# Six row buffers for the f32 expert blocks of a decoder layer, a norm diagonal on GpSimd, and key halves placed behind the norm

## The chip, the cores and the metric

The kernel runs on one core of a Trainium2 chip. What counts is device time in microseconds from start to end of one execution. The kernel before takes 1702.3 us (median of three runs, 1701.36 to 1702.61). All rows of a trace come from one other execution, run under the profiler, that took 1700.27 us; times in rows count from its first instruction.

## The reference

One decoder layer: 512 tokens, width 1024, float32, one batch. The layer mixes tokens (a gated recurrence beside a sparse attention), adds the result to the residual stream, sends the normed stream through an expert mixer with 16384 experts, of which each token uses 16 for each of 8 heads, and adds a gated embedding. Cut to what matters here:

```python
def rmsnorm(x, g):
    y = x32 * lax.rsqrt(jnp.mean(x32 * x32, axis=-1, keepdims=True) + EPS)
    return (y * g.astype(jnp.float32)).astype(x.dtype)

def peer_ffn(h, wq, sub_keys, u, v):
    def token_block(xt):                                  # 128 tokens
        q = (xt @ wq).reshape(PEER_TOKEN_BLOCK, PEER_HEADS, 2, PEER_DKEY // 2)
        s = jnp.einsum('thcd,hckd->thck', q, sub_keys)
        top_s, top_i = lax.top_k(s, PEER_TOPK)
        cand = top_s[:, :, 0, :, None] + top_s[:, :, 1, None, :]
        best_s, best_c = lax.top_k(cand.reshape(...), PEER_TOPK)
        ...                                               # expert = i1 * 128 + i2
        w = jax.nn.softmax(best_s, axis=-1)
        act = jax.nn.gelu(jnp.einsum('thkd,td->thk', u[expert], xt))
        return jnp.einsum('thk,thkd->td', w * act, v[expert])

        mixed = jnp.concatenate([o_hg, o_nsa], axis=-1)
        h = h + mixed @ w_out[i]
        h = h + peer_ffn(rmsnorm(h, ffn_norm[i]), peer_wq[i], peer_keys[i], peer_u[i], peer_v[i])
        gate = jax.nn.sigmoid(rmsnorm(h, ple_gate_norm[i]) @ ple_gate_w[i])
        h = h + (p[i] @ ple_proj[i]) * gate
```

## The kernel before, in words

The 512 tokens are four tiles of 128 (`tt` 0 to 3). A float32 product that must be exact is split: ScalarE writes a rounded high half of an operand, VectorE subtracts it from the operand to get the low half (`split`, L190), and TensorE adds up three matmuls of halves (`mm3`, L185). In the names `aTh` and `aTl` (`xTh` and `xTl` in the code) are the halves of the normed stream, `wh` and `wl` those of a chunk of the query weights, `kyh` and `kyl` those of the sub keys, `uh` and `ul` those of 128 rows of the expert table `u`, and `moh` and `mol` those of one tile of the attention output, transposed.

The work comes in stages. Up to about 347 us run the input projection, the recurrence, and the attention with most of its output projection. What the list `POST` (L73) then orders is the junction that the change edits. The letter "o" (`out_tile`, L518) transposes tile 0 of the attention output (L522), splits it, multiplies it with the output weights in two column halves of 12 matmuls, adds each half to the residual `h1` (L540) and sums its squares on ScalarE. The letter "n" (`ffn_norm`, L545) norms one tile: GpSimd computes the factor `rx` (three small instructions, L547, L180, L181), VectorE makes a 128x128 diagonal `dg` of it (L550, one buffer), TensorE multiplies the tile with it, which scales and transposes at once (L555), and ScalarE and VectorE write the halves `aTh` (L560) and `aTl` (L561).

Next, 16 steps (`hc`) multiply the normed stream with a chunk of the query weights each; at steps 0, 4, 8 and 12 a quarter of the sub keys is loaded into `kr_` and split (L940 to L943), and VectorE takes the 16 best scores of each key half. Tile 0 takes its experts one by one later; tiles 1 to 3 take all 16384 experts densely, in 128 blocks of 128 rows of `u`. Blocks 0 to 29 are worked on early. Six run after the last score; the others are spread between the one-hot matmuls (`wm`, L1036 and L1037) of three dense tiles, which turn the routing into a dense weight table (`wd`). Blocks 0 to 19 are "full": TensorE multiplies the float32 rows `ur` with the float32 stream `xf` (L834). Blocks 20 to 29 take the split rows `uh`, `ul` in three matmuls. The pool `dense` (L795) has two buffers of each name, 512 KB each, so two of `ur`, two of `uh` and two of `ul`; full blocks leave the last four empty. Loads of `ur` stand in SyncE's queue, apart from the last three of the 30, which GpSimd issues. Then the main loop runs over the 128 blocks (split rows of `u` and `v`, and for tile 0 gathered rows), and the gate ends the kernel.

Each engine works through its own instructions in order. Within a stage a scheduler lays the order by priorities; `tc.issue_after` puts instructions behind a given one.

Of the kernel before, what the change touches and what calls it, by code (L numbers as in the profile page):

```python
# [10 lines left out]
F32 = mybir.dt.float32  # L11
# [58 lines left out]
HPLAN = [("h", 0), ("h", 1), ("kv", 0), ("h", 2), ("h", 3)]  # L70
KPLAN = [("q", 0), ("k", 0), ("k", 1), ("s", 0), ("s", 1), ("s", 2), ("s", 3), ("c", 0)]
PLAN = [("b",0),("b",1),("c",),("a",3,(1,2,0),4),("p",),("a",3,(1,2,0),8),("a",3,(1,2,0),ALL),("l",0),("o",0,2),("o",0,0),("o",0,1),("a",2,(1,2,0),5),("a",2,(1,2,0),ALL),("o",0,3),("l",1),("a",1,(1,0,2),ALL),("o",1,3),("o",1,2),("a",0,(1,0,2),3),("a",0,(1,0,2),ALL),("o",1,1)]
POST = [("n",3),("o",0),("n",2),("n",1),("n",0)]  # L73
APRI = 150
XB = 6
NP = 3
# [83 lines left out]
def _body(ctx, tc, a, out, dbg=None):  # L160
# [354 lines left out]
            w.append((wh, wl))  # L515
        return w

    def out_tile(pool, pp, tag, bufs, w, hf, tt):  # L518
        src = (hv, nq)[hf]
        o = pp.tile([128, 512], F32, name=tag, bufs=bufs)  # L520
        for k in range(4):
            PE.transpose(o[:, k * 128:(k + 1) * 128], src[:, tt, k * 128:(k + 1) * 128], ident)  # L522
        mh = pool.tile([128, 4, 128], F32R, name="moh", bufs=MB)
        ml = pool.tile([128, 4, 128], F32R, name="mol", bufs=MB)
        split(flat(mh), flat(ml), o)
        outer = not hf and tt == LAST0
        os_ = [pp.tile([128, 512], F32, name=tag, bufs=bufs) for _ in range(2)] if outer else []
        for k in range(4 if outer else 0):
            for n in range(2):
                ns = slice(n * 512, (n + 1) * 512)  # L530
                mm3(os_[n], mh[:, k], ml[:, k], w[k][0][:, ns], w[k][1][:, ns], k == 0, k == 3)
        for n in range(2):
            ns = slice(n * 512, (n + 1) * 512)
            if outer:
                o = os_[n]
            else:
                o = pp.tile([128, 512], F32, name=tag, bufs=bufs)
                for k in range(4):
                    mm3(o, mh[:, k], ml[:, k], w[k][0][:, ns], w[k][1][:, ns], k == 0, k == 3)
            V.tensor_tensor(h1[:, tt, ns], h1[:, tt, ns], o, op=ALU.add)  # L540
            if hf:
                junk = pool.tile([128, 512], F32, name="junk")
                act(junk, h1[:, tt, ns], AF.Square, accum_out=ss[:, tt, n:n + 1])

    def ffn_norm(pool, pp, tag, bufs, tt):  # L545
        ts = slice(tt * 128, (tt + 1) * 128)
        G.tensor_tensor(rx[:, tt:tt + 1], ss[:, tt, 0:1], ss[:, tt, 1:2], op=ALU.add)  # L547
        rstd(rx[:, tt:tt + 1], rx[:, tt:tt + 1], 1, 1.0 / D)
        dg = pool.tile([128, 128], F32, name="dg", bufs=DGB)
        V.tensor_scalar(dg, ident, rx[:, tt:tt + 1], None, op0=ALU.mult)  # L550
        for q in range(2):
            o = pp.tile([128, 512], F32, name=tag, bufs=bufs)
            for k in range(4):
                c = 4 * q + k
                PE.matmul(o[:, k * 128:(k + 1) * 128], lhsT=h1[:, tt, c * 128:(c + 1) * 128], rhs=dg, start=True, stop=True)  # L555
            for k in range(4):
                c = 4 * q + k
                gc = gn[:, G_FFN + c:G_FFN + c + 1]
                ok = o[:, k * 128:(k + 1) * 128]
                act(xTh[:, c, ts], ok, AF.Copy, scale=gc)  # L560
                V.scalar_tensor_tensor(xTl[:, c, ts], ok, gc, xTh[:, c, ts].bitcast(F32), op0=ALU.mult, op1=ALU.subtract)  # L561

    dram = ctx.enter_context(tc.tile_pool(name="dram", bufs=1, space=DRAM))
    ppd = dram.tile([T, D], F32, name="ppd")
# [226 lines left out]
    wp = wpx.enter_context(tc.tile_pool(name="wp", bufs=2, reuse_waits="tile"))  # L791
    with ExitStack() as e2:
        ps = e2.enter_context(tc.tile_pool(name="ps2", bufs=6, space=PSUM, reuse_waits="tile"))
        for name, tt in POST:
            if name == "n":  # L795
                ffn_norm(wop, ps, "mm", 6, tt)
            else:
                out_tile(wop, ps, "mm", 6, wo_, 1, tt)
        put("h1", h1)
        wox.close()  # L800
        den = ExitStack()
        dense = den.enter_context(tc.tile_pool(name="dense", bufs=2, side="right", reuse_waits="tile"))
        pre = ExitStack()
        prep = pre.enter_context(tc.tile_pool(name="prep", bufs=AHEAD, side="right", reuse_waits="tile"))
# [14 lines left out]
    def a_steps(full):  # L819
        b = nextb[0]  # L820
        nextb[0] += 1
        dq = nc.gpsimd if NPRE - HOLD <= b < NPRE else nc.sync
        ur = dense.tile([128, NC, 128], F32, name="ur")
        dq.dma_start(out=ur, in_=a["uT"][b])
        g_ = prep.tile([128, TD], F32, name="gp") if b < AHEAD else dense.tile([128, TD], F32, name="ga", bufs=3)
        ahead.append(g_ if b < AHEAD or b >= NPRE else None)
        if not full:
            uh = dense.tile([128, NC, 128], F32R, name="uh")
            ul = dense.tile([128, NC, 128], F32R, name="ul")
            split(flat(uh), flat(ul), flat(ur))  # L830
        o = aps.tile([128, 512], F32, name="apsum")
        for c in range(NC):
            if full:
                PE.matmul(o[:, :TD], lhsT=ur[:, c], rhs=xf[:, c], start=c == 0, stop=c == NC - 1)  # L834
            else:
                mm3(o[:, :TD], uh[:, c], ul[:, c], xTh[:, c, T - TD:], xTl[:, c, T - TD:], c == 0, c == NC - 1)
            if c < NC - 1:
                yield
        act(g_, o[:, :TD], AF.Gelu_apprx_tanh)
        if AHEAD <= b < NPRE:  # L840
            dq.dma_start(out=gd[b - AHEAD], in_=g_)
# [76 lines left out]
    with ExitStack() as e2:  # L918
# [4 lines left out]
        with ExitStack() as e3:  # L923
            ps = e3.enter_context(tc.tile_pool(name="ps3", bufs=6, space=PSUM, reuse_waits="tile"))
            e3.enter_context(wpx)
            qs = []
            for hc in range(17):
                if hc == 4:
                    for c in range(NC):
                        G.tensor_tensor(xf[:, c], xTh[:, c, T - TD:].bitcast(F32), xTl[:, c, T - TD:].bitcast(F32), op=ALU.add)  # L930
                if hc < 16:
                    raw = wp.tile([128, NC, 128], F32, name="wr")
                    nc.sync.dma_start(out=raw, in_=a["wq"][:, hc])
                    wh = wp.tile([128, NC, 128], F32R, name="wh")
                    if hc == 0:
                        kyh = wp.tile([128, 16, 128], F32R, name="kyh", bufs=1)
                        kyl = wp.tile([128, 16, 128], F32R, name="kyl", bufs=1)
                    wl = wp.tile([128, NC, 128], F32R, name="wl")
                    split(flat(wh), flat(wl), flat(raw))
                    if hc % 4 == 0:  # L940
                        kr_ = wp.tile([128, 4, 128], F32, name="kr_")
                        nc.sync.dma_start(out=kr_, in_=a["keys"][:, hc:hc + 4])
                        split(kyh[:, hc:hc + 4], kyl[:, hc:hc + 4], kr_)  # L943
                    o = ps.tile([128, 512], F32, name="mm")
                    for c in range(NC):
                        mm3(o, wh[:, c], wl[:, c], xTh[:, c], xTl[:, c], c == 0, c == NC - 1)
                    qh = wp.tile([128, T], F32R, name="qh")
                    ql = wp.tile([128, T], F32R, name="ql")
                    split(qh, ql, o)
                    qs.append((qh, ql))  # L950
                if hc:
                    h = hc - 1
                    qh, ql = qs[h]
                    o = ps.tile([128, NT, 128], F32, name="mm")
                    for tt in range(NT):
                        ts = slice(tt * 128, (tt + 1) * 128)
                        last = mm3(o[:, tt], qh[:, ts], ql[:, ts], kyh[:, h], kyl[:, h], True, True)
                    for tt in range(NT):
                        V.max(tv[tt][:, h, 0:8], o[:, tt])
                        V.max_index(ti[tt][:, h, 0:8], tv[tt][:, h, 0:8], o[:, tt])  # L960
                        rep = wp.tile([128, 128], F32, name="rep")
                        V.match_replace(out=rep, in_to_replace=tv[tt][:, h, 0:8], in_values=o[:, tt], imm_value=-3e38)
                        V.max(tv[tt][:, h, 8:16], rep)
                        V.max_index(ti[tt][:, h, 8:16], tv[tt][:, h, 8:16], rep)
            with tc.issue_after(last.ins):
                for _ in range(XB):
                    a_block(True)
# [321 lines left out]
```

## Time and profile before

| What | us |
|---|---|
| median of three runs | 1702.3 |
| the profiled execution | 1700.27 |
| its span, first to last instruction | 1698.5 |
| TensorE busy / VectorE busy | 1650.0 / 1260.3 |
| ScalarE busy / GpSimd busy | 745.3 / 486.1 |

The profiled execution lies 2.0 us below the median, and 1.8 us of it are outside the span. PE is TensorE's matmuls, PEld its weight loads, DVE is VectorE, ACT is ScalarE, POOL is GpSimd and SP is SyncE. Busy shares are means over stages with different limits, so a change in one stage is read from that stage. A float32 matmul shows as more than one record in the trace: the eight of one tile's norm are the "x16" of L555.

### The profile page before, as it was taken

How to read it: one execution, taken by the hardware profiler on the slowest of the kernel's cores; microseconds unless marked ns; L12 is line 12 of the kernel's file. 1: busy time of each engine (PE TensorE's matmuls, PEld its weight loads, DVE VectorE, ACT ScalarE, POOL GpSimd, SP SyncE). 2: the span in 40 equal slices, each digit the busy share in tenths (PEclk: the TensorE clock that was granted, in tenths of full speed). 3: DMA queues.
4: the chain of work that ended last, by engine and by line, in shares of the span. 5: the costliest groups of instructions: out<-in, count | busy, mean ns of one | idle time of the engine just before them, and what ended most of it. 6: DMA issues, size and time to landing. Idle time of an engine off the chain costs nothing.

```text
span 1698.5 us, 24123 instructions
## 1 busy us (share of the span) xinstructions
PE 1650.0 (97%) x8864; PEld 1416.2 (83%) x8864; DVE 1260.3 (74%) x2485; ACT 745.3 (44%) x1291; POOL 486.1 (29%) x356
## 2 busy tenths in 40 slices
PE   9999999979999999999999999999999999999998
PEld 7887888768866668878899999999999999888987
DVE  6565745659999987865487877777878877787864
ACT  7443664652237875533333333333333333433342
POOL 0013000020000000000055655655545544455610
PEclk9999999989999999999999999999999999999999
DMA  7311130032214689967589898898898988899941
GB/s 256 112 50 49 45 100 25 26 101 86 63 50 146 203 259 287 309 222 239 171 302 327 309 337 313 323 331 325 318 324 323 322 318 322 319 329 333 328 140 50
DMA packets 148647, 373.38 MB, mean 220 GB/s; under 512 B 11990, under 2 KB 59734, under 8 KB 148526
## 3 DMA queue, kind: packets, MB, share of 16 engines
q1 hardware_dynamic: 109808, 231.46, 40.4%
q0 software_dynamic: 38720, 140.38, 23.3%
q8 instruction: 69, 1.13, 0.3%
q14 instruction: 50, 0.41, 0.1%
HBM read 339.02 MB, written 32.77 MB: 219 GB/s over the span
## 4 chain that ended last, share of the span: by engine, by line
PE 50%; issue 17%; DMA 15%; POOL 9%; DVE 5%; ACT 3%; SPq 0%; POOLq 0%; DVEq 0%; ACTq 0%
POOL row L1093 8%; DMA row<-v,eid 7%; PE ac L188 5%; PE ac L186 5%; PE ac L187 5%; PE mm L186 4%; PE mm L187 4%; PE mm L188 4%; PE apsum L834 3%; DMA ur<-uT 3%; DMA row<-u,eid 3%; PE apsum L188 3%; PE apsum L186 3%; PE apsum L187 3%; PE ob L708 2%
## 5 line engine op out<-in xcount | busy, mean ns | idle before, releaser
L188 PE MATMUL ac<-vh,pl 128*128 128x512 f32 x768 | 301.9, 394 | 1.9 <-DVE pl L192 1.7
L1093 POOL DMA_INDIRECT row<-u,eid x128 | 216.2, 1689 | 304.3 <-DVE hn L1097 246.3
L187 PE MATMUL ac<-vl,ph 128*128 128x512 f32 x768 | 301.1, 392 | 0.5 <-DVE vl L192 0.5
L186 PE MATMUL ac<-vh,ph 128*128 128x512 f32 x768 | 299.4, 391 | 1.9 <-ACT vh L191 1.0
L188 PE MATMUL apsum<-aTh,ul 128*128 128x384 f32 x864 | 290.4, 336 | 3.9 <-DVE ul L192 3.9
L186 PE MATMUL apsum<-aTh,uh 128*128 128x384 f32 x864 | 291.5, 337 | 0.5 <-ACT uh L191 0.5
L187 PE MATMUL apsum<-aTl,uh 128*128 128x384 f32 x864 | 289.6, 335 | 0.0
L1093 POOL DMA_INDIRECT row<-v,eid x128 | 208.8, 1631 | 184.0 <-DVE hn L1105 160.4
L191 ACT ACTIVATE uh<-ur 128x1024 fp32r<-128x1024 f32 x108 | 114.5, 1060 | 248.5 <-PE apsum L187 230.1
L192 DVE TENSOR_TENSOR ul<-ur,uh 128x1024 fp32r<-128x1024 f32 x108 | 132.1, 1223 | 78.5 <-ACT uh L191 78.3
L1105 DVE SCALAR_TENSOR_TENSOR hn<-row,cw__7013,hn 128x1024 f32<-128x1024 f32 x128 | 158.6, 1281 | 21.9 <-DMA row<-v,eid 21.7
L188 PEld LDWEIGHTS ac<-vh,pl 128*128 128x128 f32 x768 | 144.1, 188 | 34.8 <-DVE pl L192 4.8
L191 ACT ACTIVATE ph<-ga 128x384 fp32r<-128x384 f32 x118 | 62.0, 525 | 249.3 <-DVE ga L1154 194.6
L186 PEld LDWEIGHTS ac<-vh,ph 128*128 128x128 f32 x768 | 144.4, 188 | 30.7 <-ACT ph L191 2.2
L187 PEld LDWEIGHTS ac<-vl,ph 128*128 128x128 f32 x768 | 144.3, 188 | 29.2 <-DVE vl L192 1.2
L192 DVE TENSOR_TENSOR vl<-vr,vh 128x1024 fp32r<-128x1024 f32 x128 | 156.0, 1219 | 16.0 <-ACT vh L191 16.0
L188 PEld LDWEIGHTS apsum<-aTh,ul 128*128 128x128 f32 x864 | 162.8, 188 | 5.2 <-DVE ul L192 5.2
L191 ACT ACTIVATE vh<-vr 128x1024 fp32r<-128x1024 f32 x128 | 135.2, 1056 | 71.3 <-PE ac L188 70.4
L186 PEld LDWEIGHTS apsum<-aTh,uh 128*128 128x128 f32 x864 | 162.8, 188 | 4.5 <-ACT uh L191 0.6
L187 PEld LDWEIGHTS apsum<-aTl,uh 128*128 128x128 f32 x864 | 162.8, 188 | 3.9
L1097 DVE SCALAR_TENSOR_TENSOR hn<-row,hn 128x1024 f32<-128x1024 f32 x128 | 156.2, 1221 | 3.3 <-DMA row<-u,eid 1.8
L834 PE MATMUL apsum<-xf,ur 128*128 128x384 f32 x320 | 114.7, 503 | 9.5 <-DMA ur<-uT 9.5
(403 smaller groups left out, 2902.7 us busy)
## 6 DMA issues: line engine op xcount, KB each, us to landing
vr<-v SPq DMA_DIRECT2D x128, 512.0 KB, 5.4
ur<-uT SPq DMA_DIRECT2D x125, 512.0 KB, 6.4
xf<-wd SPq DMA_DIRECT2D x30, 768.0 KB, 8.3
wraw<-wi SPq DMA_DIRECT2D x20, 512.0 KB, 4.8
wd<-hn SPq DMA_DIRECT2D x5, 1664.0 KB, 8.7
wd<-stage SPq DMA_DIRECT2D x5, 1664.0 KB, 9.3
wr<-wq SPq DMA_DIRECT2D x16, 512.0 KB, 3.6
wor<-wo SPq DMA_DIRECT2D x16, 256.0 KB, 2.7
```

The lines of the kernel that those rows point to most:

```text
L186: PE.matmul(o, lhsT=lh, rhs=rh, start=first, stop=False)
L187: PE.matmul(o, lhsT=lh, rhs=rl, start=False, stop=False)
L188: return PE.matmul(o, lhsT=ll, rhs=rh, start=False, stop=last)
L191: act(hi, src, AF.Copy)
L192: return V.tensor_tensor(lo, src, hi.bitcast(F32), op=ALU.subtract)
L708: PE.matmul(o_ps[:, h], lhsT=pt[:, k * 128:(k + 1) * 128], rhs=kv[:, k, 256 + i * 64:256 + (i + 1) * 64], start=(k == 0), stop=(k == tt))
L834: PE.matmul(o[:, :TD], lhsT=ur[:, c], rhs=xf[:, c], start=c == 0, stop=c == NC - 1)
L1093: G.indirect_dma_start(out=gt, out_offset=None, in_=table, in_offset=bass.IndirectOffsetOnAxis(ap=eid[:, slot:slot + 1], axis=0))
L1097: V.scalar_tensor_tensor(junk, gt, 1.0, xn0, op0=ALU.mult, op1=ALU.mult, accum_out=dots[:, s_:s_ + 1])
L1105: V.scalar_tensor_tensor(ak, gt, cw_[:, s_:s_ + 1], ak, op0=ALU.mult, op1=ALU.add)
```

## The change

Four edits. The diagonal is made on GpSimd in place of VectorE. `POST` starts with a new letter "t": the transposes of tile 0 and their split (`out_turn`) come ahead of the norm of tile 3, and `out_tile` later uses their result. All four key splits are issued behind the last `aTl` of the norm. The row buffer of a full block takes the names `ur`, `uh`, `ul` in turn. (`WLP` is 99, a step that doesn't exist, so its branch is never taken.)

```diff
-POST = [("n",3),("o",0),("n",2),("n",1),("n",0)]
+DGG = 1
+KYP = 16
+WLP = 99
+POST = [("t",0),("n",3),("o",0),("n",2),("n",1),("n",0)]
...
-    def out_tile(pool, pp, tag, bufs, w, hf, tt):
+    def out_turn(pool, pp, tag, bufs, hf, tt):
         src = (hv, nq)[hf]
...
         split(flat(mh), flat(ml), o)
+        return mh, ml
+
+    def out_tile(pool, pp, tag, bufs, w, hf, tt, turned=None):
+        mh, ml = turned or out_turn(pool, pp, tag, bufs, hf, tt)
...
-        V.tensor_scalar(dg, ident, rx[:, tt:tt + 1], None, op0=ALU.mult)
+        (G if DGG else V).tensor_scalar(dg, ident, rx[:, tt:tt + 1], None, op0=ALU.mult)
...
-                V.scalar_tensor_tensor(xTl[:, c, ts], ok, gc, xTh[:, c, ts].bitcast(F32), op0=ALU.mult, op1=ALU.subtract)
+                normed[0] = V.scalar_tensor_tensor(xTl[:, c, ts], ok, gc, xTh[:, c, ts].bitcast(F32), op0=ALU.mult, op1=ALU.subtract)
...
+            elif name == "t":
+                turned = out_turn(wop, ps, "mm", 6, 1, tt)
             else:
-                out_tile(wop, ps, "mm", 6, wo_, 1, tt)
+                out_tile(wop, ps, "mm", 6, wo_, 1, tt, turned)
...
-        ur = dense.tile([128, NC, 128], F32, name="ur")
+        ur = dense.tile([128, NC, 128], F32, name=("ur", "uh", "ul")[b % 3] if full else "ur")
...
-                        split(kyh[:, hc:hc + 4], kyl[:, hc:hc + 4], kr_)
+                        if hc < KYP:
+                            with tc.issue_after(normed[0].ins):
+                                split(kyh[:, hc:hc + 4], kyl[:, hc:hc + 4], kr_)
...
```

How it moves instructions shows at three places. On TensorE, where the junction begins, the order before has the norm of tile 3 (mm_3390, mm_3403), then the transposes (mm_3416), and the two halves of the output projection (mm_3425, mm_3441) start mixed, with the norm of tile 2 (mm_3462) between them:

```order
L555 MATMUL mm_3390<-dg_3388,h1_63 128x128 x4
L555 MATMUL mm_3403<-dg_3388,h1_63 128x128 x4
L522 MATMUL mm_3416<-cst_61,hn_66 128x128 x4
L186 MATMUL mm_3425<-woh0_2683,moh_3421 128x512
L187 MATMUL mm_3425<-wol0_2684,moh_3421 128x512
L186 MATMUL mm_3441<-woh0_2683,moh_3421 128x512
L187 MATMUL mm_3441<-wol0_2684,moh_3421 128x512
L555 MATMUL mm_3462<-dg_3460,h1_63 128x128 x3
L188 MATMUL mm_3425<-woh0_2683,mol_3422 128x512
```

The same place after the change (line numbers are those of the changed kernel):

```order
L525 MATMUL mm_3385<-cst_61,hn_66 128x128 x4
L564 MATMUL mm_3399<-dg_3397,h1_63 128x128 x4
L564 MATMUL mm_3412<-dg_3397,h1_63 128x128 x4
L189 MATMUL mm_3425<-woh0_2683,moh_3390 128x512
L190 MATMUL mm_3425<-wol0_2684,moh_3390 128x512
L191 MATMUL mm_3425<-woh0_2683,mol_3391 128x512
L189 MATMUL mm_3425<-woh1_2693,moh_3390 128x512
```

The transposes lead, the 24 matmuls of the projection follow in one piece, and the norms of tiles 2, 1 and 0 stand behind them.

On VectorE, in the middle of the norm before, the low key halves (kyl, from the quarters kr__3850, kr__4142 and kr__4434) stand between the last adds of the projection (h1_63) and the low halves of the normed stream:

```order
L540 TENSOR_TENSOR h1_63<-h1_63,mm_3425 128x512
L192 TENSOR_TENSOR kyl_3583<-kr__3850,kyh_3582 128x512
L192 TENSOR_TENSOR kyl_3583<-kr__4142,kyh_3582 128x512
L540 TENSOR_TENSOR h1_63<-h1_63,mm_3441 128x512
L561 SCALAR_TENSOR_TENSOR aTl_1621<-mm_3462,gn_62,aTh_1620 128x128
L550 TENSOR_SCALAR dg_3491<-cst_61,rx_67 128x128
L561 SCALAR_TENSOR_TENSOR aTl_1621<-mm_3462,gn_62,aTh_1620 128x128
L561 SCALAR_TENSOR_TENSOR aTl_1621<-mm_3475,gn_62,aTh_1620 128x128
L192 TENSOR_TENSOR kyl_3583<-kr__4434,kyh_3582 128x512
L561 SCALAR_TENSOR_TENSOR aTl_1621<-mm_3462,gn_62,aTh_1620 128x128
```

After the change, at the norm's end on VectorE:

```order
L570 SCALAR_TENSOR_TENSOR aTl_1621<-mm_3524,gn_62,aTh_1620 128x128
L570 SCALAR_TENSOR_TENSOR aTl_1621<-mm_3537,gn_62,aTh_1620 128x128 x2
L195 TENSOR_TENSOR kyl_3583<-kr__3587,kyh_3582 128x512
L195 TENSOR_TENSOR kyl_3583<-kr__3850,kyh_3582 128x512
L195 TENSOR_TENSOR kyl_3583<-kr__4142,kyh_3582 128x512
L195 TENSOR_TENSOR kyl_3583<-kr__4434,kyh_3582 128x512
L195 TENSOR_TENSOR wl_3695<-wr_3692,wh_3694 128x1024
L195 TENSOR_TENSOR ql_3617<-mm_3591,qh_3616 128x512
```

All four key halves stand behind the norm now, ahead of the low half of the third weight chunk (wl_3695) and of the first queries (ql_3617). The four diagonals have left VectorE and stand behind `rx` on GpSimd.

In SyncE's queue, before, behind the last chunk of query weights, the row loads (ur) of blocks 2 to 9 and the first write of the weight table (wd0, wd1):

```order
L824 DMA ur_4783<-uT 128x1024
L824 DMA ur_4796<-uT 128x1024
L824 DMA ur_4809<-uT 128x1024
L824 DMA ur_4822<-uT 128x1024
L824 DMA ur_4996<-uT 128x1024
L824 DMA ur_5065<-uT 128x1024
L824 DMA ur_5169<-uT 128x1024
L1051 DMA wd0_3370<-hn_4977 128x6x128
L1052 DMA wd1_3371<-hn_4977 128x26x128
L824 DMA ur_5294<-uT 128x1024
```

After the change, behind the last chunk of query weights:

```order
L836 DMA ur_4996<-uT 128x1024
L836 DMA uh_5065<-uT 128x1024
L836 DMA ul_5169<-uT 128x1024
L836 DMA ur_5294<-uT 128x1024
L836 DMA uh_5380<-uT 128x1024
L836 DMA ul_5474<-uT 128x1024
L836 DMA ur_5581<-uT 128x1024
L1071 DMA wd0_3370<-hn_4977 128x6x128
L1072 DMA wd1_3371<-hn_4977 128x26x128
L836 DMA uh_5650<-uT 128x1024
```

The loads of blocks 0 to 5 have moved ahead, among the early weight chunks (four of them ahead of the key quarters kr__4142 and kr__4434), and four more loads stand ahead of the first table write.

## Rows read from the trace of the kernel before

**Rows 1.** The page, busy time by engine:

```profile
PE 1650.0 (97%) x8864; PEld 1416.2 (83%) x8864; DVE 1260.3 (74%) x2485; ACT 745.3 (44%) x1291; POOL 486.1 (29%) x356
```

**Rows 2.** Windows: stretch, length, busy by engine, clock, DMA share, GB/s; main loop:

```profile
900.00:1000.00 100.00, 100.00 (x508) 91.09 (x507) 78.90 (x115) 36.81 (x49) 52.74 (x32) 1.00 0.90 328
```

**Rows 3.** Chain of waits, junction: start, duration, engine or DMA, what:

```profile
358.58 0.69 DVE h L540
359.27 0.61 DVE kyl L192
...
359.95 4.18 DMA kr__4434<-keys
...
364.81 0.69 DVE kyl L192
365.50 2.29 DVE aTl L561 x9
...
368.03 0.37 DVE dg L550
...
372.23 0.43 PE mm L186
...
375.17 0.23 PE mm L186
```

**Rows 4.** Timeline of TensorE, junction: start, duration, instruction, idle before and releaser:

```profile
349.07 2.90 PE L555 MATMUL mm<-dg,h 128*128 128x128 f32 x16 [1.99 <-DVE h L540]
351.76 1.06 PE L522 MATMUL mm<-cst,hn 128*128 128x128 f32 x4
...
360.42 0.40 PE L188 MATMUL mm<-woh,mol 128*128 128x512 f32 x1
...
362.37 2.05 PE L555 MATMUL mm<-dg,h 128*128 128x128 f32 x16 [0.44 <-DVE dg L550]
368.44 3.78 PE L555 MATMUL mm<-dg,h 128*128 128x128 f32 x16 [4.02 <-DVE dg L550]
```

**Rows 5.** Windows of the junction:

```profile
349.00:353.00 4.00, 3.75 (x20) 3.35 (x20) 1.17 (x5) 2.45 (x6) 0.93 (x3) 0.63 0.00 0
364.50:368.40 3.90, 0.00 (x0) 0.00 (x0) 3.59 (x13) 3.58 (x13) 2.04 (x3) 0.84 0.32 129
368.40:372.20 3.80, 3.76 (x17) 3.76 (x18) 1.56 (x5) 1.21 (x4) 3.80 (x5) 0.50 0.00 0
```

**Rows 6.** Timeline of GpSimd, the factor of the last norm:

```profile
363.14 0.55 POOL L181 TENSOR_TENSOR rx<-rx,mhalf 128x1 f32<-128x1 f32 x1
```

**Rows 7.** Lines of GpSimd: busy, mean ns, idle before:

```profile
L670 POOL TENSOR_TENSOR pc<-pc,cst 128x256 f32<-128x256 f32 x4 | 2.9, 734 | 47.0 <-ACT pc L669 47.0
...
L180 POOL TENSOR_SCALAR rx<-rx 128x1 f32<-128x1 f32 x8 | 1.5, 191 | 27.8 <-ACT n L1179 15.3 <-ACT hn L1179 12.1
```

**Rows 8.** Windows, middle of the query-weight steps:

```profile
400.00:413.90 13.90, 13.90 (x73) 11.70 (x72) 13.69 (x69) 3.09 (x4) 0.00 (x0) 1.00 0.27 77
```

**Rows 9.** Timeline of TensorE, full blocks in a row:

```profile
484.01 23.43 PE L834 MATMUL apsum<-xf,ur 128*128 128x384 f32 x72
```

**Rows 10.** Windows, dense tiles and the tail behind them:

```profile
540.00:550.00 10.00, 7.56 (x53) 4.91 (x51) 10.00 (x20) 9.94 (x19) 0.00 (x0) 1.00 0.93 277
570.00:580.00 10.00, 8.18 (x35) 4.96 (x36) 7.22 (x42) 4.76 (x14) 0.00 (x0) 0.83 0.55 164
511.00:636.00 125.00, 115.53 (x767) 77.08 (x767) 113.19 (x280) 99.55 (x224) 0.00 (x0) 0.97 0.69 204
636.00:702.00 66.00, 61.02 (x500) 56.72 (x498) 48.48 (x69) 33.50 (x44) 6.46 (x8) 0.97 0.95 297
```

**Rows 11.** Waits 511 to 640 us: engine, line, releaser: total, times, longest:

```profile
PE apsum L834 <- DMA ur<-uT: 9.5, 5, 2.4
```

**Rows 12.** Waits 636 to 703 us:

```profile
ACT uh L191 <- DMA ur<-uT: 8.4, 4, 4.4
```

**Rows 13.** Timeline of GpSimd before the main loop:

```profile
681.88 0.54 POOL L1077 DMA_DIRECT2D hn<-fgain  x1 [4.49 <-DMA wd<-hn]
```

**Rows 14.** The page, DMA issues: count, KB each, us from issue to landing:

```profile
ur<-uT SPq DMA_DIRECT2D x125, 512.0 KB, 6.4
```

More of the change, by code (lines that the diff above doesn't have):

```diff
@@ L543, in out_tile @@
                 act(junk, h1[:, tt, ns], AF.Square, accum_out=ss[:, tt, n:n + 1])
+    normed = [None]
     def ffn_norm(pool, pp, tag, bufs, tt):
@@ L793, in _body @@
         ps = e2.enter_context(tc.tile_pool(name="ps2", bufs=6, space=PSUM, reuse_waits="tile"))
+        turned = None
         for name, tt in POST:
@@ L938, in _body @@
                     wl = wp.tile([128, NC, 128], F32R, name="wl")
-                    split(flat(wh), flat(wl), flat(raw))
+                    if hc == WLP:
+                        with tc.issue_after(normed[0].ins):
+                            split(flat(wh), flat(wl), flat(raw))
+                    else:
+                        split(flat(wh), flat(wl), flat(raw))
                     if hc % 4 == 0:
@@ L942, in _body @@
                         nc.sync.dma_start(out=kr_, in_=a["keys"][:, hc:hc + 4])
-                        split(kyh[:, hc:hc + 4], kyl[:, hc:hc + 4], kr_)
+                        if hc < KYP:
+                            with tc.issue_after(normed[0].ins):
+                                split(kyh[:, hc:hc + 4], kyl[:, hc:hc + 4], kr_)
+                        else:
+                            split(kyh[:, hc:hc + 4], kyl[:, hc:hc + 4], kr_)
                     o = ps.tile([128, 512], F32, name="mm")
```

## The prediction

> **What bounds the kernel now.** I read the busy times first: TensorE works 1650.0 of 1698.5 us [rows 1]. The windows then say where it has no gap at all: in the main loop it is busy 100.00 us of 100 at clock 1.00, with VectorE at 78.90 and the DMA engines at 0.90 [rows 2]. So the loop keeps its length whatever comes before it, and a microsecond that TensorE gains or loses ahead of about 700 us reaches the end, unless a transfer or another engine takes it back on the way. The query-weight steps are just as dense, TensorE 13.90 of 13.90, but there VectorE has 13.69 of 13.90 [rows 8]: nothing can be gained in them and little may be added to VectorE. Gaps of TensorE that the four edits touch lie in two places: the junction at 349 to 379 us, which I read in the chain of waits and the timeline, and the dense tiles at 511 to 636 us, read in the waits and windows.
>
> **The junction.** The chain runs h, a low key half, the load of a key quarter (4.18 us, as its buffer comes free with that half), another low key half at 364.81, nine aTl (2.29), and only then the last diagonal at 368.03 [rows 3]. Its factor rx had been ready since 363.14 + 0.55 = 363.7 [rows 6]. VectorE, working in order, thus held the diagonal 4.3 us, and TensorE stood idle 4.02 us before the last norm [rows 4]. In that idle stretch the granted clock fell to a mean of 0.84, and the next stretch ran at 0.50, that is 1.2 GHz [rows 5]: the last norm took 3.78 us where the one before it took 2.05 [rows 4], and the first query matmuls came every 0.43 us in place of 0.23 [rows 3].
>
> Now the same place after the change, step by step. The start stays at 349.07, since it waits for h. The four transposes (1.06) come first and end at 350.1, the norm of tile 3 (2.90, at a mean clock of 0.63 [rows 5], which I keep) at 353.0. Beside that norm the two splits of the transposed tile go through ScalarE and VectorE, about 0.69 each by the low key half of the same size [rows 3], so they are done near 351.5 and the projection need not wait. Its 24 matmuls at 0.233 take 5.6 and end at 358.6, where they ended at 360.42 + 0.40 = 360.8 [rows 4]. The norm of tile 2 takes 2.05: 360.7. With one buffer for the diagonal, the next one is made when the last norm is through. A 128x128 TENSOR_SCALAR on GpSimd is not in this trace. Its nearest rows are the 128x1 TENSOR_SCALAR (191 ns) below and a 128x256 op with two inputs (734 ns) above [rows 7]; I take 0.4 us, since it has one input and half those elements, and 0.2 for the passage to TensorE. So the norm of tile 1 ends at 360.7 + 0.6 + 2.05 = 363.3, that of tile 0 at 366.0. The last factor is no later: it followed the projection's end by 363.7 - 360.8 = 2.9, which gives 361.5. The gaps are 0.6 us in place of 4.02, so I keep the clock at full.
>
> The first 24 query matmuls ended before at 372.23 + 4 x 0.43 + 0.30 + 19 x 0.233 = 378.7 (the 0.30 is my reading of the step between the two rates). After the change they need 5.6, and about 1.0 of waiting for the last halves aTh and aTl, which trail the norm: 366.0 + 6.6 = 372.6, or 6.1 earlier.
>
> What is late next are the keys. VectorE ends aTl near 367 and takes two key halves (0.69 each, to 368.4); two more quarters can only be loaded then, 4.18 us, and their high and low halves end near 374.6. The low half of the third weight chunk and the first low queries stand behind them on VectorE, about 1.4 and 0.69 by their sizes, done near 376.7. They are needed when step 1 ends, at 372.6 + 5.6 = 378.2, with 1.5 us to spare; a landing over 5.7 us costs one for one. I book +0.6. SyncE's queue holds the fifth weight chunk behind those loads and six row loads, but that is wanted only four steps on. The junction then gives -6.1 + 0.6 = **-5.5**.
>
> Its bounds: if the clock stays at 0.50 through the last norm and the first queries, 1.7 and about 1.3 are lost again, and two diagonals at 0.73 cost 0.7 more: -2. With the small diagonal (0.19), without the wait for halves or the +0.6: -7.5.
>
> The Trainium skill has a rule against the diagonal's move: GPSIMD Engine Reference, section "8. Key points", says that for elementwise work VectorE is about twice as fast. By it the diagonal would be twice the 0.37 us that it took on VectorE [rows 3], an estimate of 0.74 each, and the junction would give -4.8. No row here shows this operation on both engines, and the sum above doesn't use it.
>
> **The dense tiles.** From 511 to 636 us TensorE is busy 115.53 of 125 [rows 10]; the 9.47 us of idle time is the 9.5 us for which full blocks wait for their rows [rows 11]. A block runs 23.43/4.5 = 5.21 us alone (72 records, 16 a block) [rows 9], and a load takes 6.4 from issue to landing [rows 14], more where the queue is full. With two buffers the load of block b+2 can only start when block b has ended. With six it starts four blocks earlier, and the first six are in before the stage begins, when the DMA engines were at 0.27 [rows 8]. So I take it that the waits for rows go. The clock's mean of 0.97 in the stage costs at most 125 x 0.03 = 3.75. The ceiling is then 9.5 + 3.75 = 13.2.
>
> Not all of it comes. In 540 to 550 TensorE is busy 7.56, and the 2.4 missing is one of the waits for rows; yet VectorE is busy 10.00 of 10 there [rows 10], making one-hots. If the rows come earlier, TensorE waits for the one-hots in its place: that 2.4 isn't gained. In 570 to 580 VectorE has 7.22 and the clock 0.83, so 1.7 us of rate are lost to a clock that fell in a gap; that comes back. 9.5 - 2.4 + 1.7 = 8.8. VectorE has 113.19 us of work in the 125 [rows 10]; after a gain of 8.8 it would be at 97%, so I take off 1.8 for short new waits on it: **-7**. The floor is 0 (VectorE or the DMA queue takes all), the ceiling 13.2.
>
> The tail, 636 to 702 us, moves 297 GB/s at a DMA share of 0.95 [rows 10]. Its split blocks still take two buffers of ur, and its end is a chain from the weight table through GpSimd's loads [rows 13], which no edit shortens. I book 0; it could give 2.5 of its 66 - 61.02 = 5 us idle or lose 3, if row and table transfers meet closer together.
>
> **Sum.** The profiled execution took 1700.3: 1700.3 - 5.5 - 7.0 = 1687.8. It lies 2.0 below the median of the runs, so on their footing 1689.8, **1690**. The likeliest case's own bounds are about 1684 to 1695.
>
> **Rivals.**
> (a) Something else takes the place of the waits for rows. For it: VectorE at 10.00 of 10 in part of the stage, ScalarE at 9.94, the DMA engines at 0.93 [rows 10]; a ring that is refilled sooner asks the same engines for the same bytes in less time. Against: all idle time of TensorE in the stage is released by a row load, and over the whole 125 us VectorE has 11.8 to spare. The stage gives 1, the junction 5.5: 1702.3 - 6.5 = 1696.
> (b) The key quarters land late or the clock stays low at the junction: it gives 2, the dense tiles 7: 1702.3 - 9 = 1693. For it: four row loads, 2 MB, now stand directly ahead of those quarters in SyncE's queue. Against: they can start once the projection weights are done with at 358.6, and the quarters not before 368.4.
> (c) The change doesn't do what it says: the scheduled gaps go but both places stay bound elsewhere, by (a) and (b) together. 1702.3 - 2 - 1 = 1699.
> (d) Slower. In the tail ScalarE and VectorE hold their split work in order, and the changed order has the splits of block 20 and those after it earlier, ahead of one-hot and table work. Each row load that is late then blocks both engines, and TensorE behind them. Today ScalarE waits 8.4 us for four rows, the longest 4.4 [rows 12]. If all seven blocks that SyncE feeds cost 4.4, that is 31, or 22 more: 1702.3 - 12.5 + 22 = 1712. It decides from 8.4 + 12.5 = 20.9 us of such waits on. For it: the DMA share of 0.95. Against: ScalarE has 33.50 of 66 in the tail and can wait without being late.
>
> **How the numbers follow.** Forecast 0.60, (a) 0.20, (b) 0.06, (c) 0.07, (d) 0.07. The range 1682 to 1699 holds the forecast, (a), (b) and half of (c), and leaves out the slower case and the deepest end (a ceiling of 13.2 with 7.5 gives 1682 before any tail gain). What this kernel's measurement can tell from no change is about 0.2%, 3.4 us. Faster by more: forecast, (a) and (b), 0.86. Within it: (c), 0.07. Slower: 0.07.
>
> **What would show it.** Right: the last diagonal on GpSimd under 0.7 us and TensorE's gap before the last norm under 1 us; the last norm near 2.05 us and the clock at 1.00 behind it; the first query matmuls near 367 us; waits of L834's counterpart for rows under 3 us in the dense tiles, and that stage some 7 us shorter. Wrong: a wait for kyl or ql in the first three query steps; the waits for rows replaced by waits for one-hots of the same sum; a main loop that starts less than 10 us earlier than at 702 us though both stages got shorter, which would put the loss into the tail; or a new gap in the loop itself, which would overturn the first paragraph.

## The result, and the profile after

The changed kernel takes 1685.9 us (median of four runs, 1683.3 to 1689.0) against 1701.8 for the kernel before (four runs, 1699.8 to 1702.6): a ratio of 0.9913, 95% interval 0.9898 to 0.9928, that is 12 to 17 us faster. Forecast were 1690 and the range 1682 to 1699. The profiled execution took 1683.29 us, its span fell from 1698.5 to 1681.5.

The first line of the page after, and then TensorE's timeline at the places that bound the stages (columns as in [rows 4]):

```profile
PE 1644.2 (98%) x8864; PEld 1411.5 (84%) x8864; DVE 1260.7 (75%) x2481; ACT 744.3 (44%) x1291; POOL 493.2 (29%) x360
```

```profile
349.79 0.66 PE L525 MATMUL mm<-cst,hn 128*128 128x128 f32 x4 [2.00 <-DVE h L547]
350.29 1.95 PE L564 MATMUL mm<-dg,h 128*128 128x128 f32 x16
...
357.55 1.95 PE L564 MATMUL mm<-dg,h 128*128 128x128 f32 x16
360.33 2.05 PE L564 MATMUL mm<-dg,h 128*128 128x128 f32 x16 [0.83 <-POOL dg L559]
363.22 2.05 PE L564 MATMUL mm<-dg,h 128*128 128x128 f32 x16 [0.84 <-POOL dg L559]
365.48 0.50 PE L189 MATMUL mm<-aTh,wh 128*128 128x512 f32 x1 [0.21 <-DVE aTl L570]
...
377.85 0.33 PE L189 MATMUL mm<-kyh,qh 128*128 128x128 f32 x1
...
379.23 0.33 PE L191 MATMUL mm<-kyh,ql 128*128 128x128 f32 x1 [0.94 <-DVE ql L195]
...
380.40 0.45 PE L189 MATMUL mm<-aTh,wh 128*128 128x512 f32 x1
...
479.02 5.38 PE L846 MATMUL apsum<-xf,ur 128*128 128x384 f32 x16
...
622.53 0.42 PE L189 MATMUL apsum<-aTh,uh 128*128 128x384 f32 x1
...
681.79 0.34 PE L191 MATMUL apsum<-aTh,ul 128*128 128x384 f32 x1
...
685.87 1.59 PE L189 MATMUL ac<-vh,ph 128*128 128x512 f32 x5 [3.75 <-ACT vh L194]
```

The same bounds in the trace of before (the first full block and the first matmul of the junction are in [rows 9] and [rows 4]):

```profile
385.39 0.45 PE L186 MATMUL mm<-aTh,wh 128*128 128x512 f32 x1
...
637.70 0.42 PE L186 MATMUL apsum<-aTh,uh 128*128 128x384 f32 x1
...
701.06 0.34 PE L188 MATMUL apsum<-aTh,ul 128*128 128x384 f32 x1
702.36 1.41 PE L186 MATMUL ac<-vh,ph 128*128 128x512 f32 x5 [0.96 <-ACT vh L191]
```

Their differences give the stages. The junction runs here from its first matmul to the first of the third weight chunk (the last row of 380.40 and 385.39), the dense stage from the first full to the first split block.

| us | before | after | difference |
|---|---|---|---|
| start of the junction | 349.07 | 349.79 | +0.7 |
| junction | 36.32 | 30.61 | -5.7 |
| remaining query steps | 98.62 | 98.62 | 0 |
| dense stage | 153.69 | 143.51 | -10.2 |
| split blocks, to the main loop | 64.66 | 63.34 | -1.3 |
| main loop and gate | 996.1 | 995.6 | -0.5 |

The start lies between 347.8 and 351.1 in the executions below, ahead of everything that was changed, and the main loop varies by some us too, so I compare stages.

In the junction TensorE's gaps before the norms of tiles 2, 1 and 0 are now none, 0.83 and 0.84 (before: none, 0.44 and 4.02), and the last norm takes 2.05, before 3.78 [rows 4]. What is late next shows in the chain of waits after the norm:

```profile
369.61 2.31 DVE kyl L195 x2
371.98 3.73 DMA kr__4434<-keys
...
376.27 1.05 ACT wh L194
377.35 0.52 DVE wl L195
...
378.50 0.69 DVE ql L195
```

The last key quarter loads only when the first halves are done. The third weight chunk and the low queries follow it, and TensorE waits 0.94 us for the low queries.

In the dense tiles the waits for rows [rows 11] are gone. The two windows that match, first of before and then of after, and TensorE's waits after, all of them:

```profile
511.00:637.70 126.70, 117.23 (x786) 78.30 (x785) 114.39 (x280) 100.04 (x225) 0.00 (x0) 0.98 0.70 206
```

```profile
506.00:622.50 116.50, 114.83 (x784) 77.46 (x784) 113.15 (x280) 99.48 (x226) 0.00 (x0) 0.99 0.70 206
```

```profile
PE wm L1005 <- DVE f32i L1002: 4.1, 2, 3.3
PE wm L1006 <- DVE f32i L1003: 0.8, 1, 0.8
```

TensorE's idle time falls from 9.47 to 1.67, that is by 7.8 us, and its busy time by 2.4, as the clock fell less. Of the waits 3.3 us lie just ahead of the tiles, as before. The other two, 0.83 and 0.84, are the 1.67: TensorE waits for VectorE, which writes the routing of the second dense tile (`f32i`). They lie in the first dense tile, as the first wait for rows did. TensorE, first before and then after:

```profile
510.75 0.47 PE L985 MATMUL wm<-cst,f32i 128*128 128x128 f32 x1 [3.31 <-DVE f32i L982]
...
546.27 2.20 PE L834 MATMUL apsum<-xf,ur 128*128 128x384 f32 x6 [2.44 <-DMA ur<-uT]
...
561.51 0.27 PE L987 MATMUL wm<-cst,ew 128*128 128x128 f32 x1
```

```profile
505.77 0.33 PE L1005 MATMUL wm<-cst,f32i 128*128 128x128 f32 x1 [3.31 <-DVE f32i L1002]
...
548.23 0.30 PE L1005 MATMUL wm<-cst,f32i 128*128 128x128 f32 x1 [0.83 <-DVE f32i L1002]
...
555.88 0.33 PE L1006 MATMUL wm<-cst,f32i 128*128 128x128 f32 x1 [0.84 <-DVE f32i L1003]
```

The last matmul shown of before comes at 556.05 in the changed kernel. So the first dense tile, from the first of these rows on, got only 0.5 us shorter (50.76 to 50.28); the other 9.7 us come from the two tiles behind it.

### The profile page after: what moved, and what is told of

It is laid out like the page before. It is cut to its first block, busy times and chain, and to the rows that moved or that the text cites. A ratio compares the mean times of both kernels' runs of the same rounds, so it can differ in the third digit from the quotient of the medians.

```text
span 1681.5 us, 24125 instructions
## 1 busy us (share of the span) xinstructions
PE 1644.2 (98%) x8864; PEld 1411.5 (84%) x8864; DVE 1260.7 (75%) x2481; ACT 744.3 (44%) x1291; POOL 493.2 (29%) x360
## 4 chain that ended last, share of the span: by engine, by line
PE 53%; issue 16%; DMA 11%; DVE 9%; POOL 8%; ACT 2%; SPq 0%; POOLq 0%; DVEq 0%; ACTq 0%
DMA row<-v,eid 8%; POOL row L1113 6%; PE ac L191 6%; PE ac L190 6%; PE ac L189 6%; PE apsum L189 4%; PE apsum L191 4%; PE apsum L190 4%; PE mm L191 4%; PE mm L189 4%; PE mm L190 4%; PE apsum L846 3%; PE ob L717 2%; PE pt L714 1%; DMA row<-u,eid 1%
## 5 line engine op out<-in xcount | busy, mean ns | idle before, releaser
L195 DVE TENSOR_TENSOR pl<-ga,ph 128x384 fp32r<-128x384 f32 x118 | 65.8, 558 | 72.9 <-ACT ph L194 72.8
```

Of the source, the lines that this page charges most:

```text
L195: return V.tensor_tensor(lo, src, hi.bitcast(F32), op=ALU.subtract)
```

## The experiments

All stand beside runs of the kernel before on the same chip.

**The ring alone.** The changed kernel with `DGG = 0`, `KYP = 0` and the old `POST`:

```diff
-DGG = 1
-KYP = 16
-POST = [("t",0),("n",3),...]
+DGG = 0
+KYP = 0
+POST = [("n",3),...]
```

> The six row buffers alone; the junction as in the kernel before (norm of tile 3 ahead of the transposes, diagonal on VectorE, key halves where the scheduler puts them). Theory A (the two halves of the change add up): the first full block starts near 484 us as before, the dense tiles (from the end of the six blocks to the first split block) shorten from 127 to 116.5 with waits for rows under 1 us, the early split blocks take 59 in place of 63, the main loop starts near 691, about 1691 us. Theory B (they lean on each other): the row loads, now ahead of two key quarters in the queue, hold up VectorE's key half in the old junction, so the junction is 2 to 4 us longer than before and the time about 1694. Theory C (the dense tiles got shorter because the stage began at another moment): waits for rows of some 4 us or more stay, time 1697.

1688.5 us, ratio 0.9919 (0.9902 to 0.9937). The junction takes 36.6, the dense stage 143.6 and the split blocks 63.2: theory A. The old junction was not held up further (B), and no wait for rows is left (C). A's 59 for the split blocks was missed: they end 62.2 after their start, before 63.7.

**The junction alone.**

```diff
-        ur = dense.tile([128, NC, 128], F32, name=("ur", "uh", "ul")[b % 3] if full else "ur")
+        ur = dense.tile([128, NC, 128], F32, name="ur")
```

> The changed kernel with two row buffers again. Theory A: junction as in the changed kernel (query matmuls end some 5 to 6 us earlier than before, first full block near 479), then 9 to 10 us of waits for rows in the dense tiles and a stage of 127 us, split blocks 63; about 1696 us. Theory C: the dense tiles stay short without the ring (under 120 us), about 1688.

1693.2 us, ratio 0.9958 (0.9943 to 0.9973), 3 us less than A had. The junction takes 30.0, the dense stage 154.2 and the split blocks 64.3. The wait for rows is back as it was, though the stage begins earlier, so A holds and not C:

```profile
PE apsum L846 <- DMA ur<-uT: 9.8, 5, 2.4
```

By the stages the parts add up (10.1 + 1.5 - 0.3 for the ring, 6.3 - 0.5 + 0.4 for the junction, 17.5 in all; the whole change gives 17.2). By the medians they sum to 21 where the change gave 16, with intervals 5 to 6 us wide; the stages decide here.

**The diagonal back on VectorE.**

```diff
-DGG = 1
+DGG = 0
```

> The changed kernel with the four diagonals on VectorE. Theory K (the key half with its load was the stall, and moving the keys is enough): TensorE's gap before the last norm stays under 1.5 us, the clock at full, the diagonal takes 0.3 in place of 0.6; time within 1 us of the changed kernel (1686). Theory D (the engine is what counts, since the last diagonal still stands behind low halves of the norm of tile 1): gap of 3 to 4 us, the last norm at half clock, 1690.

1684.6 us, ratio 0.9906 (0.9886 to 0.9925): by its time no different from the changed kernel. The junction takes 31.8, 1.2 more than in the changed kernel's profile. Seven executions with the junction of the changed kernel take 29.9 to 31.3, so 1.2 is little more than their spread. Half of each theory held. The last norm and the low queries on TensorE:

```profile
364.61 3.68 PE L564 MATMUL mm<-dg,h 128*128 128x128 f32 x16 [3.02 <-DVE dg L559]
...
380.06 0.33 PE L191 MATMUL mm<-kyh,ql 128*128 128x128 f32 x1 [0.41 <-DVE ql L195]
```

The gap and the slow norm return (D), since the diagonal stands behind low halves of tile 1 on VectorE, and the first query matmul starts 18.6 us after the start of the junction, not 15.7. But the keys were going to be late anyway, and the wait for low queries shrinks from 0.94 to 0.41: more than half of the 2.9 us is hidden again.

**The keys left free.**

```diff
-KYP = 16
+KYP = 0
```

> The changed kernel with the key splits where the scheduler puts them, the diagonal still on GpSimd. Theory K: VectorE waits for the load of a key quarter inside the norm again, its low halves come late, and TensorE waits 2 to 4 us for them (or for a PSUM buffer): 1689. Theory D: the gap before the last norm stays under 1 us, the wait for the first low queries (0.9 us in the changed kernel) goes as the keys are done early, 1685.

1684.5 us, ratio 0.9899 (0.9880 to 0.9919); junction 31.8. As D had it, the gap before the last norm stays at 0.84 and no wait for low queries is left; as K had it, TensorE waits for halves, 1.66 us before the first query matmul. So, beside the rest, moving the keys and moving the diagonal are worth some 1.2 us each by the profiles, at most 2 by the spread named above, and nothing that the times show.

**Without the early transposes.**

```diff
-POST = [("t",0),("n",3),("o",0),("n",2),("n",1),("n",0)]
+POST = [("n",3),("o",0),("n",2),("n",1),("n",0)]
```

> The changed kernel without the early transposes (norm of tile 3 first, as before). Theory K (the low queries, late behind the key quarters, set the junction's end): TensorE gets a gap of about 1.5 us again before the projection, but the wait for the low queries shrinks by as much; from the first transposes or norm to the third chunk of query matmuls 30.6 to 31.3 us (30.6 in the changed kernel, 36.3 before), time within 1 us of the changed kernel. Theory T (each gap of TensorE in the junction counts in full): 32 us, +1.5 us.

1689.6 us, ratio 0.9950 (0.9933 to 0.9967); junction 34.6, so 4.0 more. Both theories expected less. TensorE and then the window behind its gap:

```profile
351.57 0.60 PE L525 MATMUL mm<-cst,hn 128*128 128x128 f32 x4
354.30 0.50 PE L189 MATMUL mm<-woh,moh 128*128 128x512 f32 x1 [2.12 <-ACT moh L194]
```

```profile
354.30:358.00 3.70, 3.70 (x13) 3.19 (x14) 3.14 (x8) 2.81 (x6) 0.00 (x0) 0.57 0.52 152
```

The gap of 2.12 is followed by a projection at a clock of 0.57, which over 3.70 us costs another 1.6. Of the junction's three edits the early transposes thus weigh most. In all three executions without them the clock fell behind one of two gaps: before behind the first, of 1.99, where the norm of tile 3 took 2.90 [rows 4]; here and with the ring alone behind the second, of 2.12, while that norm took 2.02 and 2.05. In the eleven executions with them the second gap is gone, and behind the first, 1.98 to 2.00 long, the norm took 1.95.

**Four row buffers, in two orders.** The name of a full block's buffer, in two separate runs:

```diff
-name=("ur", "uh", "ul")[b % 3] if full else "ur"
+name=("ur", "uh")[b % 2] if full else "ur"
...
-name=("ur", "uh", "ul")[b % 3] if full else "ur"
+name=("ur", "ur", "uh")[b % 3] if full else "ur"
```

The second was meant to be a ring of three. But each name has two buffers, so full blocks have four there too: one named `ur` comes back after three blocks, one named `uh` after six.

> Full blocks over four row buffers in place of six. Theory R (the waits for rows fall with each buffer, as loads queue among the table writes): 1 to 4 us of waits for rows remain, from the first full block to the first split one 145 to 148 us (143.5 with six, 153.7 with two), time 1687 to 1690. Theory S (a load of 6.4 us fits in one block and its one-hots, so two more buffers are enough): waits under 0.5 us, 143.5 us, as the changed kernel.

> Full blocks over three row buffers. Two left 9.5 us of waits for rows, four left none. Theory S (one more load in flight is what was missing): waits under 1 us, 143.5 to 145 us from the first full to the first split block. Theory R (each buffer takes its share): 3 to 6 us of waits, 147 to 150.

The first order: 1683.4 us, ratio 0.9909 (0.9893 to 0.9926), dense stage 143.6, no wait for rows: S. The second, one execution of 1688.3: 143.6 as well and no wait for rows in TensorE's full blocks, so it was enough that two loads of three can start three blocks ahead. A ring of three buffers was not run. In the second order the split blocks take 71.8 in place of 63.3. Their start there, and then with six buffers:

```profile
620.60:640.00 19.40, 15.23 (x150) 14.11 (x148) 16.96 (x16) 10.25 (x12) 0.00 (x0) 0.84 1.03 306
```

```profile
622.50:640.00 17.50, 17.50 (x166) 16.55 (x164) 16.22 (x15) 10.93 (x13) 0.00 (x0) 1.00 1.06 325
```

In this order the last two full blocks, 18 and 19, sit in both `ur` buffers, and the split blocks behind them load into no other. With six buffers block 19 has `uh`. That this causes it I read from the names; no run took it apart.

**More work for VectorE.** Three one-hot products of the first dense tile are written twice.

```diff
-                V.tensor_tensor(oh, o1, bc(wh), op=ALU.mult)
+                for _ in range(2 if tt == 1 and k in (2, 3, 4) else 1):
+                    V.tensor_tensor(oh, o1, bc(wh), op=ALU.mult)
```

> The changed kernel with three one-hot products (1.2 us each) of the first dense tile written twice, the same values: 3.6 us more of work for VectorE in a stretch where it is busy all the time. Theory F (VectorE is the next bound there, right behind the row loads): TensorE's wait for the routing of the second dense tile grows from 0.8 to 3 us or more, and the stage from first full to first split block from 143.5 to 146 to 147. Theory G (VectorE runs well ahead of TensorE): stage 143.5 to 144.

One execution, 1687.3 us, dense stage 146.7: 3.2 of the 3.6 us added. TensorE's waits:

```profile
PE wm L1005 <- DVE f32i L1002: 4.9, 2, 3.3
PE wm L1006 <- DVE f32i L1003: 2.0, 2, 1.5
```

The stage is as F expected (the eleven other executions without waits for rows take 143.5 to 144.6). The waits are so only in part: 2.0 us more, of which the second tile's routing has 0.4 and the third's 1.5. The other 1.2 us are busy time of TensorE at a lower clock behind the gap of 3.3 us, which lies ahead of the added work. The changed kernel and then this one, 3 to 6 us behind the end of that gap:

```profile
508.77:511.77 3.00, 3.00 (x10) 1.72 (x9) 3.00 (x5) 1.13 (x4) 0.00 (x0) 0.89 0.16 18
```

```profile
509.99:512.99 3.00, 3.00 (x6) 1.54 (x5) 3.00 (x5) 0.12 (x1) 0.00 (x0) 0.58 0.00 0
```

TensorE waits for VectorE later in that tile in both kernels, so I take it that at full clock it would have waited so much longer; no run shows that. VectorE is the next bound, right behind the rows.

**v rows ahead of u rows.** The two row loads of blocks 30 and 31 are put behind the first load of v:

```diff
+    vfirst = [None]
...
-        dq.dma_start(out=ur, in_=a["uT"][b])
+        if NPRE <= b < NPRE + 2:
+            with tc.issue_after(vfirst[0].ins):
+                dq.dma_start(out=ur, in_=a["uT"][b])
+        else:
+            dq.dma_start(out=ur, in_=a["uT"][b])
...
+            vfirst[0] = vfirst[0] or vdma[0]
```

> The changed kernel with the first load of v rows issued ahead of the two u-row loads of blocks 30 and 31. Theory V (the 3.75 us gap before the main loop is the queue order: v rows wait behind u-row loads that wait for buffers): gap under 1 us, the main loop starts 3 us earlier after the last split block, time 1683. Rival (the DMA engines at a share of 0.99 are the bound, the order only deals out the same bytes): the gap stays 2.5 us or more, or the last split blocks end later by what the gap loses; time within 1 us of 1686.

1688.0 us, ratio 0.9932 (0.9914 to 0.9951): not faster. The gap before the first matmul goes, and a longer one opens behind it:

```profile
683.02 0.40 PE L189 MATMUL ac<-vh,ph 128*128 128x512 f32 x1
688.69 0.79 PE L190 MATMUL ac<-vl,ph 128*128 128x512 f32 x1 [5.28 <-DVE vl L195]
```

The low half of the same rows stands behind the routing of tile 0 on VectorE. Behind that gap the clock was 0.50 for 4.86 us, which costs another 2.4. V was right on the queue and wrong on the time: another wait lay behind it.

**Two attempts to go further.** The first edit alone, then both; and the changed kernel again beside the latter.

```diff
-                        if hc < KYP:
+                        if 8 <= hc < KYP:
...
-DGB = 1
+DGB = 2
```

> Only the third and fourth key quarters are split behind the norm; the first two go where the scheduler puts them, so the loads of the last two can start inside the norm. Theory K: the wait for low queries (0.94 us) and the 4 us load behind the norm go, the gap before the last norm stays under 1 us; junction 29.4 us in place of 30.6, time about 1 us under the changed kernel (within what a run tells). Rival: as with all keys left free, low halves of the norm come late and TensorE waits 1 to 2 us before the first query matmul: junction 31.5.

> Only the third and fourth key quarters behind the norm, and two buffers for the diagonal, so that it can be made while the norm before still runs. Theory P (TensorE's two gaps of 0.84 us in the norm are what is left): they go, junction 28.5 us, time 2 us under the changed kernel. Theory Q (ScalarE and VectorE, which write the halves of the normed stream, are the bound there): the first query matmuls wait for those halves by what the gaps lose; junction 29.9 as with late keys alone, time 1 us under the changed kernel or the same.

> The changed kernel once more, unaltered, to stand beside the next one on the same chip. Both theories: 1684 to 1687 us; junction 30.6 us, from the first full block to the first split one 143.5.

| | median us | ratio to before | junction |
|---|---|---|---|
| late keys only | 1679.5 | 0.9881 (0.9865 to 0.9898) | 30.0 |
| and two diagonals | 1681.9 | 0.9892 (0.9870 to 0.9915) | 29.1 |
| changed, again | 1684.2 | 0.9896 (0.9873 to 0.9919) | 30.3 |

With late keys the wait for low queries goes, as K expected. But the gap before the last norm grows to 1.61, which K had under 1: on GpSimd the last diagonal now stands behind a product of 1.00 for `xf`. And TensorE waits 0.73 for halves before the first query matmul, less than the rival had. With two diagonals one of the two gaps goes and the first query matmuls wait for halves, between P and Q. Both medians lie under that of the changed kernel's second set of runs, by 5 and 2 us (the first was taken on another occasion). The junction explains 0.3 and 1.2 of it, and the intervals overlap, so neither is shown to beat the changed kernel.

## Why the prediction was right, and where it was off

**The main loop carries a shift to the end: right.** It kept its length to 0.5 us. That closeness is luck in part: in the other executions whose edit ends ahead of it the loop takes 994.2 to 999.2.

**The junction, -5.5: right in sum, -5.7, not in its parts.** Its errors cancelled: up to the first score matmul it gave 7.0, where I had 6.1, and the keys took 1.3 back, where I had 0.6. The transposes and the norm of tile 3 ran at full clock (0.66 and 1.95 where I had 1.06 and 2.90), so the projection ended 3.8 us earlier after the start, not 2.2. The diagonal took 0.60 to 0.62, not 0.4, and its gaps 0.84, not 0.6. The wait for halves was as I had it, about 1: two chunks took 377.85 - 365.48 = 12.4 where 48 x 0.233 = 11.2. From the first score to the third chunk it now takes 2.55 us, before 1.28; the wait for `ql` in it, 0.94, is the one of my signs of being wrong that came. I had made the diagonal's stall the heart of it; in the runs the early transposes weigh 4.0, diagonal and keys 1.1 to 1.2 each.

**The dense tiles, -7: the mechanism right, the gain too small, -10.2.** Every wait for rows went. I had taken off 2.4, because VectorE was at 10.00 of 10 beside one of them, and 1.8 more for short waits on VectorE. The first was nearly right: in the same tile TensorE now waits 1.67 for VectorE, for routing and not for one-hots, and that tile gained only 0.5. The term that failed is the 1.8: no further wait came, though VectorE is now busy 113.15 of 116.50, the 97% from which I had worked it out. The clock gave 2.4 back where I had 1.7. So 9.47 - 1.67 + 2.4 = 10.2.

**The tail, 0: -1.3.** The split blocks end 4.1 us earlier after their start (59.6 in place of 63.7), TensorE being 57.0 busy of 59.3 at full clock, and 2.8 of that goes back in the gap before the main loop (3.75 in place of 0.96). I had left that gap out. The ring alone ends them 1.5 earlier, the junction alone 0.1; where the rest comes from stays open.

**The rivals.** (a) did not happen; its VectorE has the 1.67. (b) is the 1.3 of the keys, small. (c) and (d) did not happen: in the tail one wait for rows of 5.8 us on ScalarE is left in place of four with 8.4, far from 20.9. The profiled execution took 1683.3 where I had 1687.8. The dense tiles' 3.2 and the tail's 1.3 make up these 4.5; the other differences cancel.

## What to carry to other kernels

Read the idle time of the bounding engine in a stage by its releasers: if one transfer ends all of it, the gain of removing it is that idle time plus the clock it lost, less what the next releaser takes. Look for the next releaser in the window of each wait: VectorE, busy 10.00 of 10 beside one of them, took 1.67 of its 2.44 back, while a mean share of 97% over the stage cost nothing more. How close it stands is measured by adding work to it. At a junction a stall's length is not its worth: with the diagonal back on VectorE the queries started 2.9 us later, and the junction was 1.2 longer, as another wait stood behind. So price the whole chain and take edits out one by one. A gap just ahead of a dense run can be paid nearly twice where the clock falls behind it (2.12 and then 1.6).

## What the runs showed of the hardware

VectorE's subtraction of two operands in SBUF, the on-chip memory, slowed down beside GpSimd. In the changed kernel GpSimd computes xf while VectorE splits the first keys. GpSimd's timeline, then VectorE's:

```profile
359.67 0.60 POOL L559 TENSOR_SCALAR dg<-cst,rx 128x128 f32<-128x128 f32 x1 [6.71 <-PE mm L564]
...
363.13 8.24 POOL L942 TENSOR_TENSOR xf<-aTh,aTl 128x384 f32<-128x384 f32 x8
```

```profile
369.53 0.96 DVE L195 TENSOR_TENSOR kyl<-kr__3587,kyh 128x512 fp32r<-128x512 f32 x1
370.42 1.50 DVE L195 TENSOR_TENSOR kyl<-kr__3850,kyh 128x512 fp32r<-128x512 f32 x1
374.12 0.69 DVE L195 TENSOR_TENSOR kyl<-kr__4142,kyh 128x512 fp32r<-128x512 f32 x1 [2.20 <-ACT kyh L194]
```

The two that began before xf ended at 371.37 took 0.96 and 1.50, those after it 0.69. With the diagonal on VectorE xf ended at 369.26, ahead of the first key half, and all four took 0.68 to 0.69. With late keys only, one beside xf took 1.60. Not each one is slowed: without the early transposes two lay beside xf, and they took 0.68 and 1.51. So moving the keys behind the norm put them beside xf, which is part of why they were late. The Trainium skill (SBUF — State Buffer, section "SBUF: two separate sides") says that a VectorE operation with two SBUF inputs and a GpSimd operation that reads SBUF take turns on one pair of ports, the second waiting for the first to end. The trace agrees: a subtraction lost 0.3 to 0.9 us, no more than one of the eight products for xf takes, about 1.0.

The diagonal of 128x128 took 0.60 to 0.62 us on GpSimd. On VectorE it took 0.28 to 0.29, and 0.36 and 0.54 where GpSimd was at work on xf. So GpSimd took about twice as long, and more than the 0.4 that I had assumed. The prediction's estimate by the Trainium skill (GPSIMD Engine Reference, section "8. Key points") was 0.74.

A gap of 2 us in TensorE's work left the clock at full in some executions (2.00 us in the changed kernel, then the transposes at full rate) and low in others (1.99 us before, then 0.63 [rows 5]; 2.12 us without the early transposes, then 0.57).
